# Output projection of a hybrid encoder layer on one Trainium2 core: where two weight blocks, two scale rows and the last two kept units are loaded, and in which order they are split

## The chip, the cores and the metric

The kernel runs on one core of one Trainium2 chip, in one launch. Times are device microseconds. A core has five engines with a queue each: TensorE (PE in the profile, its weight loads PEld), VectorE (DVE), ScalarE (ACT), GpSimd (POOL) and SyncE (SP). Loads and stores are issued here by SP and by POOL; 16 DMA engines carry them out. An instruction starts when its turn in its engine's queue has come and the semaphores that it waits for are reached.

## The reference

One layer of a streaming encoder for 384 tokens (256 of a new stream, 8 x 16 of running streams), in three token blocks of 128. All numbers are float32. The part around the change:

```python
merged = (gates[:, :, 0] * br_pool + gates[:, :, 1] * br_ssd).astype(u.dtype)
out = merged @ p['w_out']                      # (384 x 2048) @ (2048 x 2048)
...
x = x + rmsnorm(m, p['g_mix_post'])            # m is out
hdn = jnp.square(jax.nn.relu(rmsnorm(x, p['g_mlp_pre']) @ p['w_up'])) @ p['w_down']
x = x + rmsnorm(hdn, p['g_mlp_post'])
```

`merged` comes out of a pooling branch and a state-space branch; the change touches neither. It lies between the last product of those branches (`w_ssd`) and the first of the MLP (`w_up`).

## The kernel before

**Precision.** Every float32 product is done as three products of rounded parts: a weight tile `w` is split into a high part `wh` (ScalarE, a copy) and a low part `wl` (VectorE, the difference), and so are the tokens' tiles. `mm` issues high by high, high by low, low by high (L151 to L153; L1208 to L1210 in the blocks). A split of a 128 x 1024 weight tile is one instruction of ACT and one of DVE behind it.

**The output projection** has four blocks of 512 columns.

- Block 2 is computed plainly by `moving` (L142): eight units `wo2_0` to `wo2_7` of 1024 columns, each loaded by SP into a `w` buffer, split, and multiplied with all three token blocks, 18 matmuls a unit.
- Blocks 0 and 1 are computed together by `seven` (L1177), in two calls, one for each half of the inner dimension. It replaces eight block products by seven on sums of blocks. Four weight blocks of 1 MB (W11, W12, W21, W22, called `W[0]`, `W[3]`, `W[2]`, `W[4]` in the code, loads `o_w` from `w_os`) and two sums of them (`wsum`, DVE) are split in halves named a to g; the sums of the token tiles (`S0` to `S7`, loads `w_S` from `s_scr`, by `ssplit`) go in on the other side. `evict` brings results to `hm`, and in the second call `settle` squares them (ACT) and scales them with the gain row (DVE).
- Block 3 is again plain: units `wo3_0` to `wo3_2` ahead of the second `seven`, and `wo3_3` to `wo3_7` kept: split by `keep` into tiles `eh`, `el` of pool `phk` at the end of the second `seven`, and multiplied after it for one token block after the other, 6 matmuls a unit and block. `finish3` then squares, norms (`postnorm`) and adds the residual `x1`; ahead of the last two units of the third token block eight transposes of the new `x1` stand in TensorE's queue (`first_turns`).

**Buffers.** Pool `wpool` has three buffers for each of `w`, `wh` and `wl`. A load into `w` waits until the split of the tile three loads earlier is done; a split into `wh` and `wl` waits until TensorE has left the tile three splits earlier. Units, `S` tiles and the MLP's weights take turns in `w`. `phs` (`px`) holds the six blocks, two split tiles and the splits of S; it is closed in the second `seven`, and `pg0` and `phk` take its memory, tile by tile as the last readers leave.

**What sets the order.** The engines' queues hold the instructions in an order that a scheduler finds from the program; `behind(x)` (`issue_after`) puts what follows behind instruction `x` in that order, `later()` behind the last split. TensorE's order is chained by `last[0]`. `fetch[0]` is the last unit load of `wfetch` (L64).

**Lines that the change touches.** `gains` (L1122) loads a gain row of 512 to all partitions through POOL and scales it by -0.5 on ACT; for blocks 0 and 1 it puts the row into unused parts of `hm` (L1330), for 2 and 3 into the tile `gpo`. `prep` (L1148) loads a block through POOL, `prep_late` (L1151) through SP: W21 behind unit 3 of block 2 and W22 behind unit 4 (hooks, L1326 and L1327). `seven` from L1273 opens `phk`, splits the first three kept units, settles, evicts (L1285), then loads and splits the last two (L1289), and settles again. `second` (L1341) runs the second `seven`.

Of the kernel before, what the change touches and what calls it, by code (L numbers as in the profile page):

```python
# [6 lines left out]
F32 = mybir.dt.float32  # L7
# [7 lines left out]
P = 128  # L15
# [18 lines left out]
def build(ctx, tc, io):  # L34
# [23 lines left out]
    def behind(ins):  # L58
        return nullcontext() if ins is None else tc.issue_after(ins.ins)
# [4 lines left out]
    def wfetch(src, name):  # L64
        w = wpool.tile([P, 1024], F32, tag="w", name=f"w_{name}")
        fetch[0] = sy.dma_start(w, src)
        return w, name
# [69 lines left out]
    def keep(tile, f):  # L137
        w, name = f
        h, l = tile
        return s.activation(h, w, AF.Copy), v.tensor_tensor(l, w, h.bitcast(F32), ALU.subtract)  # L140
# [901 lines left out]
    with tc.tile_pool(name="phf", bufs=1, side="right", reuse_waits="tile") as pf, tc.tile_pool(  # L1042
# [77 lines left out]
            lo(range(4), False)  # L1120

        def gains(nb, gpo=None):  # L1122
            if gpo is None:
                gpo = pf2.tile([P, 512], F32, tag="gpo", name=f"gpo{nb}", bufs=1)
            gp.dma_start(gpo, io["g_mix_post"][blk(nb)].partition_broadcast(P))
            s.activation(gpo, gpo, AF.Copy, scale=-0.5)
            return gpo

# [21 lines left out]

        def prep_late(i):  # L1151
            with behind(fetch[0]):
                sy.dma_start(W[(0, 3, 2, 4)[i]], io["w_os"][0, i])

        def wsum(out, a, b):
            for q in both:
# [20 lines left out]
        def seven(c):  # L1177
# [34 lines left out]
            def settle():  # L1212
                with behind(low[0]), behind(high[0]):
                    while due:
                        b, j, src = due.pop(0)
                        squared(b, j, src)
                        scaled(b, j, src, gains01[j])
# [55 lines left out]
            if c:  # L1273
                phs.close()
                pg0 = xin.enter_context(tc.tile_pool(name="pg0", bufs=1, reuse_waits="tile"))
                xtiles(pg0, NE)
                pk = phk.enter_context(tc.tile_pool(name="phk", bufs=1, reuse_waits="tile"))
                for i in reversed(range(5)):
                    kept[i] = [pk.tile([P, 1024], F32R, name=f"e{n}_wo3_{3 + i}") for n in "hl"]
                with behind(low[0]):  # L1280
                    for i in range(3):
                        high[0], low[0] = keep(kept[i], kf[i])
            run(g1, (2, 3), (X, 2, False))
            settle()
            evict(0, 0, X, first=True, done=True)  # L1285
            if c:
                with behind(low[0]):
                    for i in (3, 4):
                        _, low[0] = keep(kept[i], wfetch(*tail3[i]))  # L1289
            settle()  # L1290

        def finish3(b):
# [25 lines left out]
        def added(*w):  # L1318
            def go():
                with later():  # L1320
                    wsum(*w)

            return go

        hooks = {k: (lambda k=k: ssplit(k)) for k in range(4)}
        hooks[3] = lambda: (ssplit(3), prep_late(2))  # L1326
        hooks[4] = lambda: prep_late(3)  # L1327
        hooks[5] = added(1, 0, 3)
        moving(o, [(io["w_out"][0, kp], f"wo2_{kp}") for kp in range(8)], ms_, 0, done2, hook=hooks)
        gains01 = [gains(0, hm[:, 2, blk(3)]), gains(1, hm[:, 1, blk(3)])]  # L1330
        seven(0)
        blocks(1)
        for i in range(4):
# [7 lines left out]
        def second():  # L1341
            with later():
                wsum(5, 1, 4)
            kf.extend(wfetch(*u) for u in tail3[:3])
            with behind(fetch[0]):
                for b in range(3):
                    sy.dma_start(x1[:, b, :], io["x_tok"][b])
            seven(1)
            gpo3.append(gains(3))
# [563 lines left out]
```

## Time and profile before

| | |
|---|---|
| time, median of 3 runs | 2614.03 us (2613.3 to 2614.59) |
| the profiled execution: its own time | 2614.43 us |
| the profiled execution: span, first to last instruction | 2612.7 us |
| granted TensorE clock, mean | 0.999 |
| DMA, mean | 177 GB/s |
| plain units of block 2 | 1514.3 to 1547.1 us |
| first and second `seven` with units 0 to 2 of block 3 between | 1547.1 to 1615.8 us |
| kept units of block 3, for three token blocks | 1615.8 to 1639.4 us |

A line of the profile names the engine, the line of the kernel, the operation and output<-input, with buffer numbers left out: `wl_wo` is the low part of any plain unit of blocks 2 and 3, `el_wo` that of a kept unit, `o_w` any of the weight blocks, `w_S` a token sum, `trm` a transpose. SPq marks an issue of a load by SP; how long the load took is told apart from it, as us from issue to landing. In a timeline each line has start, duration, and in brackets how long the engine was idle ahead of it and who released it.

### The profile page before, as it was taken

What the parts mean: (1) busy time and instruction counts of PE and PEld (TensorE: products, weight loads), DVE (VectorE), ACT (ScalarE), POOL (GpSimd) and SP (SyncE); (2) the same over time, 40 slices, a digit from 0 to 9 for tenths busy, and PEclk for the clock granted to TensorE, in tenths of its full rate; (3) what the DMA queues carried; (4) which work ended last, traced back from release to release, by engine and by line L of the source; (5) the groups of instructions that cost most, each with busy time, mean ns of one, the idle gap of its engine ahead of it and who ended that gap; (6) DMA issues with size and microseconds to landing.
All of it is one profiled execution on the core that took longest, in us unless ns stands there. A gap on an engine that the chain in (4) does not pass through costs nothing.

```text
span 2612.7 us, 40398 instructions
## 1 busy us (share of the span) xinstructions
PE 2598.7 (99%) x15977; PEld 2500.8 (96%) x15977; DVE 1827.1 (70%) x2468; ACT 1323.4 (51%) x2008; POOL 196.7 (8%) x284
## 2 busy tenths in 40 slices
PE   9999999999999999999999999999999999999998
PEld 9999999999999999999999988999999999999997
DVE  6685334788888888876544468766676868677677
ACT  6443324666566565744333345645454545454454
POOL 0000000001111111120100000000000000000000
PEclk9999999999999999999999999999999999999999
DMA  7444445566766576666655565543433444444444
GB/s 284 143 136 155 149 146 203 183 205 208 232 210 223 198 240 201 218 215 233 215 172 167 165 213 186 217 138 129 142 132 129 157 158 142 141 146 137 137 143 144
DMA packets 139886, 463.28 MB, mean 177 GB/s; under 512 B 17712, under 2 KB 44912, under 8 KB 125232
## 3 DMA queue, kind: packets, MB, share of 16 engines
q1 hardware_dynamic: 115536, 321.99, 38.3%
q0 software_dynamic: 24160, 138.70, 14.6%
q8 instruction: 126, 2.06, 0.3%
q14 instruction: 64, 0.52, 0.1%
HBM read 412.88 MB, written 47.75 MB: 176 GB/s over the span
## 4 chain that ended last, share of the span: by engine, by line
PE 95%; DVE 1%; DMA 1%; ACT 1%; issue 1%; SPq 0%; DVEq 0%; POOL 0%; ACTq 0%; POOLq 0%
PE pj_up L101 6%; PE pj_up L102 6%; PE pj_up L103 6%; PE pj_x L101 5%; PE pj_x L103 4%; PE pj_x L102 4%; PE pj_sp L103 3%; PE pj_sp L102 3%; PE pj_sp L101 3%; PE pj_z L103 3%; PE pj_z L102 3%; PE pj_z L101 3%; PE X L1619 2%; PE c L1619 2%; PE c L1618 2%; PE c L1617 2%
## 5 line engine op out<-in xcount | busy, mean ns | idle before, releaser
L101 PE MATMUL pj_up<-x1h,wh_up 128*128 128x384 f32 (+1 forms) x1024 | 333.9, 326 | 0.0
L103 PE MATMUL pj_up<-x1h,wl_up 128*128 128x384 f32 (+1 forms) x1024 | 333.7, 326 | 0.0
L102 PE MATMUL pj_up<-x1l,wh_up 128*128 128x384 f32 (+1 forms) x1024 | 333.7, 326 | 0.0
L101 PE MATMUL pj_x<-xgh,wh_x 128*128 128x384 f32 x768 | 251.9, 328 | 0.0
L103 PE MATMUL pj_x<-xgh,wl_x 128*128 128x384 f32 x768 | 250.5, 326 | 0.3 <-DVE wl_x L74 0.3
L102 PE MATMUL pj_x<-xgl,wh_x 128*128 128x384 f32 x768 | 250.4, 326 | 0.0
L73 ACT ACTIVATE wh_up<-w_up 128x1024 fp32r<-128x1024 f32 x126 | 133.1, 1056 | 186.7 <-PE pj_up L102 110.7
L74 DVE TENSOR_TENSOR wl_up<-w_up,wh_up 128x1024 fp32r<-128x1024 f32 x126 | 154.0, 1223 | 57.7 <-ACT wh_up L73 56.9
L102 PEld LDWEIGHTS pj_up<-x1l,wh_up 128*128 128x128 f32 x1024 | 193.5, 189 | 0.4
L101 PEld LDWEIGHTS pj_up<-x1h,wh_up 128*128 128x128 f32 x1024 | 193.5, 189 | 0.4
L103 PEld LDWEIGHTS pj_up<-x1h,wl_up 128*128 128x128 f32 x1024 | 193.5, 189 | 0.0
L103 PE MATMUL pj_z<-xgh,wl_z 128*128 128x384 f32 x512 | 167.0, 326 | 0.2 <-DVE wl_z L74 0.2
L101 PE MATMUL pj_sp<-abh,wh_sp 128*128 128x384 f32 x512 | 166.9, 326 | 0.0
L102 PE MATMUL pj_sp<-abl,wh_sp 128*128 128x384 f32 x512 | 166.9, 326 | 0.0
L103 PE MATMUL pj_sp<-abh,wl_sp 128*128 128x384 f32 x512 | 166.9, 326 | 0.0
L102 PE MATMUL pj_z<-xgl,wh_z 128*128 128x384 f32 x512 | 166.9, 326 | 0.0
L101 PE MATMUL pj_z<-xgh,wh_z 128*128 128x384 f32 x512 | 166.9, 326 | 0.0
L73 ACT ACTIVATE wh_x<-w_x 128x1024 fp32r<-128x1024 f32 x96 | 100.9, 1052 | 107.0 <-PE pj_z L102 53.0
L74 DVE TENSOR_TENSOR wl_x<-w_x,wh_x 128x1024 fp32r<-128x1024 f32 x96 | 117.4, 1223 | 52.7 <-ACT wh_x L73 52.7
L74 DVE TENSOR_TENSOR wl_sp<-w_sp,wh_sp 128x1024 fp32r<-128x1024 f32 x64 | 78.3, 1223 | 108.4 <-ACT wh_sp L73 108.4
L73 ACT ACTIVATE wh_sp<-w_sp 128x1024 fp32r<-128x1024 f32 x64 | 67.8, 1059 | 166.3 <-PE pj_sp L102 158.2
L101 PEld LDWEIGHTS pj_x<-xgh,wh_x 128*128 128x128 f32 x768 | 145.1, 189 | 2.3 <-issue 0.4
(583 smaller groups left out, 7190.4 us busy)
## 6 DMA issues: line engine op xcount, KB each, us to landing
w_up<-w_up SPq DMA_DIRECT2D x128, 512.0 KB, 3.4
w<-w_dn POOLq DMA_DIRECT2D x60, 1024.0 KB, 5.2
w_x<-w_in SPq DMA_DIRECT2D x96, 512.0 KB, 4.0
w_z<-w_in SPq DMA_DIRECT2D x64, 512.0 KB, 3.5
w_sp<-w_ssd SPq DMA_DIRECT2D x64, 512.0 KB, 3.5
w_ga<-w_ga SPq DMA_DIRECT2D x32, 512.0 KB, 3.5
w_pp<-w_pp SPq DMA_DIRECT2D x32, 512.0 KB, 3.4
hs<-ssm POOLq DMA_DIRECT2D x16, 1024.0 KB, 7.2
```

The lines of the kernel that those rows point to most:

```text
L73: cut[0] = s.activation(h, w, AF.Copy)
L74: cut[1] = v.tensor_tensor(l, w, h.bitcast(F32), ALU.subtract)
L101: te.matmul(out, wh, xh, start=first, stop=False, **how)
L102: te.matmul(out, wh, xl, start=False, stop=False, **how)
L103: return te.matmul(out, wl, xh, start=False, stop=last, **how)
L1617: te.matmul(o, h[:, t], vh, start=go, stop=False, skip_group_check=True)
L1618: te.matmul(o, h[:, t], vl, start=False, stop=False, skip_group_check=True)
L1619: last[0] = te.matmul(o, l[:, t], vh, start=False, stop=False, skip_group_check=True)
```

## The change

1. W21 and W22 of the first `seven` are no longer loaded behind units 3 and 4 of block 2, but both behind unit 5's hook, and `prep_late` now moves `fetch[0]`, so that each load stands behind the one before.
2. The gain rows of blocks 0 and 1 are loaded in `second`, ahead of the loads of kept units 3 to 5, through SP and behind `fetch[0]`, no longer through POOL during the plain units.
3. The last two kept units, `wo3_6` and `wo3_7`, get `w` tiles of their own in `phk`, loaded when `phk` is opened, where they took `w` buffers of `wpool` before.
4. In the second `seven` the `settle` between the last products and the last eviction is left out, so the two last splits stand directly behind that eviction, and the rest is settled after them.

```diff
         def gains(nb, gpo=None):
+            src = io["g_mix_post"][blk(nb)].partition_broadcast(P)
             if gpo is None:
                 gpo = pf2.tile([P, 512], F32, tag="gpo", name=f"gpo{nb}", bufs=1)
-            gp.dma_start(gpo, io["g_mix_post"][blk(nb)].partition_broadcast(P))
+                gp.dma_start(gpo, src)
+            else:
+                with behind(fetch[0]):
+                    sy.dma_start(gpo, src)
             s.activation(gpo, gpo, AF.Copy, scale=-0.5)
             return gpo
...
         def prep_late(i):
             with behind(fetch[0]):
-                sy.dma_start(W[(0, 3, 2, 4)[i]], io["w_os"][0, i])
+                fetch[0] = sy.dma_start(W[(0, 3, 2, 4)[i]], io["w_os"][0, i])
...
                     kept[i] = [pk.tile([P, 1024], F32R, name=f"e{n}_wo3_{3 + i}") for n in "hl"]
+                for i in (3, 4):
+                    w = pk.tile([P, 1024], F32, name=f"w_wo3_{3 + i}")
+                    sy.dma_start(w, tail3[i][0])
+                    kf.append((w, tail3[i][1]))
                 with behind(low[0]):
                     for i in range(3):
                         high[0], low[0] = keep(kept[i], kf[i])
             run(g1, (2, 3), (X, 2, False))
-            settle()
+            if not c:
+                settle()
             evict(0, 0, X, first=True, done=True)
             if c:
                 with behind(low[0]):
                     for i in (3, 4):
-                        _, low[0] = keep(kept[i], wfetch(*tail3[i]))
+                        _, low[0] = keep(kept[i], kf[i])
             settle()
...
-        hooks[3] = lambda: (ssplit(3), prep_late(2))
-        hooks[4] = lambda: prep_late(3)
-        hooks[5] = added(1, 0, 3)
+        sum0 = added(1, 0, 3)
+        hooks[5] = lambda: (sum0(), prep_late(2), prep_late(3))
...
-        gains01 = [gains(0, hm[:, 2, blk(3)]), gains(1, hm[:, 1, blk(3)])]
+        gains01 = []
...
             with later():
                 wsum(5, 1, 4)
+            gains01[:] = [gains(0, hm[:, 2, blk(3)]), gains(1, hm[:, 1, blk(3)])]
             kf.extend(wfetch(*u) for u in tail3[:3])
```

TensorE's queue holds the same instructions in the same order. The other engines' queues move at three places.

SP during the plain units of block 2 (`wo2`), up to the first units of block 3 (`wo3`). Before:

```order
L1161 DMA w_S2_15768<-s_scr2_165 128x640
L66 DMA w_wo2_5_15774<-w_out 128x1024
L1153 DMA o_w21_0_15672<-w_os 128x2048
L1161 DMA w_S3_15798<-s_scr3_166 128x640
L66 DMA w_wo2_6_15805<-w_out 128x1024
L1153 DMA o_w22_0_15671<-w_os 128x2048
L66 DMA w_wo2_7_15830<-w_out 128x1024
L66 DMA w_wo3_0_16119<-w_out 128x1024
L66 DMA w_wo3_1_16125<-w_out 128x1024
L66 DMA w_wo3_2_16131<-w_out 128x1024
```

With the change:

```order
L1165 DMA w_S2_15768<-s_scr2_165 128x640
L66 DMA w_wo2_5_15774<-w_out 128x1024
L1165 DMA w_S3_15798<-s_scr3_166 128x640
L66 DMA w_wo2_6_15804<-w_out 128x1024
L66 DMA w_wo2_7_15828<-w_out 128x1024
L1157 DMA o_w21_0_15672<-w_os 128x2048
L1157 DMA o_w22_0_15671<-w_os 128x2048
L66 DMA w_wo3_0_16115<-w_out 128x1024
L66 DMA w_wo3_1_16121<-w_out 128x1024
L66 DMA w_wo3_2_16127<-w_out 128x1024
L1129 DMA hm_15661<-g_mix_post 128x512 x2
```

W21 (`o_w21`) and W22 (`o_w22`) have moved from behind units 5 and 6 of block 2 to behind its last unit, and the two gain rows (`hm<-g_mix_post`), on POOL before, stand behind unit 2 of block 3.

ACT at the same place; `oc`, `ob` and `oa` are the first splits of the first `seven`, `st1` takes the sums of squares. Before:

```order
L1164 ACTIVATE Sh2_15770<-w_S2_15768 128x640
L1126 ACTIVATE gpo2_15678<-gpo2_15678 128x512
L1126 ACTIVATE hm_15661<-hm_15661 128x512
L73 ACTIVATE wh_wo2_5_15776<-w_wo2_5_15774 128x1024
L1126 ACTIVATE hm_15661<-hm_15661 128x512
L1164 ACTIVATE Sh3_15800<-w_S3_15798 128x640
L73 ACTIVATE wh_wo2_6_15807<-w_wo2_6_15805 128x1024
L73 ACTIVATE wh_wo2_7_15832<-w_wo2_7_15830 128x1024
L1195 ACTIVATE wh_oc0_0_15909<-o_w1_0_15674 128x1024
L1195 ACTIVATE wh_ob0_0_15931<-o_w21_0_15672 128x1024
L1134 ACTIVATE hm_15661,st1_15662<-wo2_0_15681 128x512
```

With the change:

```order
L1168 ACTIVATE Sh2_15770<-w_S2_15768 128x640
L1130 ACTIVATE gpo2_15678<-gpo2_15678 128x512
L73 ACTIVATE wh_wo2_5_15776<-w_wo2_5_15774 128x1024
L1168 ACTIVATE Sh3_15800<-w_S3_15798 128x640
L73 ACTIVATE wh_wo2_6_15806<-w_wo2_6_15804 128x1024
L73 ACTIVATE wh_wo2_7_15830<-w_wo2_7_15828 128x1024
L1199 ACTIVATE wh_oc0_0_15905<-o_w1_0_15674 128x1024
L1199 ACTIVATE wh_ob0_0_15927<-o_w21_0_15672 128x1024
L1130 ACTIVATE hm_15661<-hm_15661 128x512 x2
L1138 ACTIVATE hm_15661,st1_15662<-wo2_0_15681 128x512
L1138 ACTIVATE hm_15661,st1_15662<-wo2_1_15682 128x512
L1138 ACTIVATE hm_15661,st1_15662<-wo2_2_15683 128x512
```

The two scalings of the gain rows (`hm<-hm`) have moved from around unit 5 to ahead of the evictions of block 2.

DVE at the end of the second `seven`, from the third kept split on; `n0` to `n3` are the small tiles of the first token block's norm, `up` the MLP's first weights. Before:

```order
L140 TENSOR_TENSOR el_wo3_5_16449<-w_wo3_5_16225,eh_wo3_5_16448 128x1024
L1130 TENSOR_TENSOR hm_15661<-oB_15905,hm_15661 128x512
L1130 TENSOR_TENSOR hm_15661<-hm_15661 128x512
L1224 TENSOR_TENSOR hm_15661<-hm_15661,oX1_16230 128x512
L140 TENSOR_TENSOR el_wo3_6_16447<-w_wo3_6_16471,eh_wo3_6_16446 128x1024
L1018 TENSOR_TENSOR n0_n10_16515<-st1_15662 128x1
L1019 TENSOR_TENSOR n0_n10_16515<-n0_n10_16515,st1_15662 128x1
L1020 TENSOR_SCALAR n0_n10_16515<-n0_n10_16515 128x1
L140 TENSOR_TENSOR el_wo3_7_16445<-w_wo3_7_16475,eh_wo3_7_16444 128x1024
L1130 TENSOR_TENSOR hm_15661<-hm_15661 128x512
L74 TENSOR_TENSOR wl_up0_0_16676<-w_up0_0_16673,wh_up0_0_16675 128x1024
L1022 TENSOR_SCALAR n1_n10_16516<-st1_15662,n0_n10_16515 128x1
```

With the change:

```order
L140 TENSOR_TENSOR el_wo3_5_16449<-w_wo3_5_16225,eh_wo3_5_16448 128x1024
L1228 TENSOR_TENSOR hm_15661<-hm_15661,oX1_16230 128x512
L140 TENSOR_TENSOR el_wo3_6_16447<-w_wo3_6_16454,eh_wo3_6_16446 128x1024
L140 TENSOR_TENSOR el_wo3_7_16445<-w_wo3_7_16456,eh_wo3_7_16444 128x1024
L1134 TENSOR_TENSOR hm_15661<-oB_15901,hm_15661 128x512
L1134 TENSOR_TENSOR hm_15661<-hm_15661 128x512 x2
L1018 TENSOR_TENSOR n0_n10_16515<-st1_15662 128x1
L74 TENSOR_TENSOR wl_up0_0_16676<-w_up0_0_16673,wh_up0_0_16675 128x1024
L1019 TENSOR_TENSOR n0_n10_16515<-n0_n10_16515,st1_15662 128x1
L74 TENSOR_TENSOR wl_up1_0_16682<-w_up1_0_16679,wh_up1_0_16681 128x1024
L1020 TENSOR_SCALAR n0_n10_16515<-n0_n10_16515 128x1
L74 TENSOR_TENSOR wl_up0_1_16688<-w_up0_1_16685,wh_up0_1_16687 128x1024
```

The eviction of the last products and the splits of units 6 and 7 have moved ahead of the settling of the rest; all three splits of the MLP's first weights stand ahead of the norm's next step, `n1`, where before one stood ahead of it, one ahead of the reciprocal, and one behind the residuals. On ACT the splits and settlings stand in the matching order, and on SP the loads of units 6 and 7 keep their place, behind the `x1` rows and ahead of the `w_up` loads.

## The prediction

> **What bounds the kernel now.** First the page, busy time by engine, beside the span in the table above.
>
> ```profile
> PE 2598.7 (99%) x15977; PEld 2500.8 (96%) x15977; DVE 1827.1 (70%) x2468; ACT 1323.4 (51%) x2008; POOL 196.7 (8%) x284
> ```
>
> TensorE is busy for all but 14 us of the span, and the change leaves its instructions and their order as they are. Time can only come from places where TensorE stands still. The second view is the list of its waits, cut to the output projection and what follows it, 1505 to 1660 us (releaser, us in total, times, longest).
>
> ```profile
> PE wo L152 <- DVE el_wo L140: 1.5, 2, 0.8
> PE wo L152 <- DVE wl_wo L74: 0.8, 1, 0.8
> PE trm L1080 <- DVE x L1065: 0.5, 1, 0.5
> ```
>
> Three places: a weight split in the plain units (wl_wo), two in the kept units (el_wo), and one transpose. From 1652 us to the end the same view is empty. The third view, busy time by stretch, gives the size. I cut it at the first matmul of block 2's plain units (1514.30), of the seven products (1547.10), of the kept units (1615.80), and behind the last kept unit.
>
> ```profile
> 1514.30:1547.10 32.80, 31.61 (x146) 27.15 (x145) 17.91 (x22) 14.93 (x20) 2.15 (x4) 1.00 0.80 279
> 1547.10:1615.80 68.70, 68.70 (x319) 60.01 (x318) 63.04 (x64) 41.21 (x54) 2.66 (x5) 1.00 0.42 154
> 1615.80:1639.40 23.60, 21.32 (x99) 17.59 (x99) 20.14 (x38) 11.72 (x22) 0.96 (x2) 1.00 0.65 222
> ```
>
> The columns are length, busy PE, PEld, DVE, ACT, POOL, granted clock, DMA share, GB/s. Plain units: 1.19 us idle, at a DMA share of 0.80. The seven products: none. Kept units: 2.28 us idle. The clock is 1.00 throughout, so a gap costs its own length. The real loss is larger than the idle time, since a matmul's modelled 0.38 us hides part of a gap; I measure from start to start, against the undisturbed 0.216 us (68.70 us for 319 recorded matmuls). A plain unit is 18 matmuls, 3.89 us; a kept unit is 6 for each token block, 1.30 us.
>
> **The first stall, unit 6 of block 2.** TensorE's timeline, then SP's issues, ACT's split of that unit, and the DMA view of 1519 to 1537 us (KB each, median us from issue to landing).
>
> ```profile
> 1537.41 0.38 PE L153 MATMUL wo<-wh_wo,ml 128*128 128x512 f32 x1
> 1538.19 0.48 PE L151 MATMUL wo<-wh_wo,mh 128*128 128x512 f32 x1 [0.41 <-ACT wh_wo L73]
> 1539.45 0.48 PE L152 MATMUL wo<-wl_wo,mh 128*128 128x512 f32 x1 [0.78 <-DVE wl_wo L74]
> 1539.77 0.38 PE L153 MATMUL wo<-wh_wo,ml 128*128 128x512 f32 x1
> ```
>
> ```profile
> 1520.79 0.33 SPq L1161 DMA_DIRECT2D w_S<-s_scr  x1
> 1521.53 0.33 SPq L66 DMA_DIRECT2D w_wo<-w_out  x1
> 1521.90 0.51 SPq L1153 DMA_DIRECT2D o_w<-w_os  x1
> 1525.48 0.33 SPq L1161 DMA_DIRECT2D w_S<-s_scr  x1
> 1530.50 0.33 SPq L66 DMA_DIRECT2D w_wo<-w_out  x1
> ```
>
> ```profile
> 1537.08 1.06 ACT L73 ACTIVATE wh_wo<-w_wo 128x1024 fp32r<-128x1024 f32 x1 [2.31 <-DMA w_wo<-w_out]
> ```
>
> ```profile
> o_w<-w_os SPq DMA_DIRECT2D x2, 1024.0 KB, 10.0
> w_S<-s_scr SPq DMA_DIRECT2D x2, 320.0 KB, 8.3
> hm<-g_mix_post POOLq DMA_DIRECT2D x2, 256.0 KB, 8.5
> ```
>
> Three steps take 2.36 us instead of 0.65: **1.71 us lost**. Followed back: ACT split unit 6 at 1537.08, when it landed, 6.6 us after its issue at 1530.50. It was issued that late because it takes the buffer of S2, and S2, issued at 1520.79, needed some 8 us, with two scale rows (256 KB each, POOL, 8.5 us) and a weight block (1 MB, SP, 1521.90, 10 us) in flight beside it.
>
> The change takes just these loads out. From S2's issue to its landing there remain the scale row of block 2, unit 5 and S2 itself, 1.1 MB instead of 2.6; at this stretch's 279 GB/s that is 4 us instead of 9. I take S2 landed at 1525, its split done by 1526.6, unit 6 issued there and landed at 1533.2 at the latest (its 6.6 us again). Its two splits (1.06 and about 1.2 us) end by 1535.6. TensorE wants unit 6 at 1514.30 + 6 x 3.89 = 1537.6, 2 us later, so the whole 1.71 us go. Bounds: 0 (S2 stays late) and 1.71.
>
> What is late next: the two weight blocks, W21 and W22, now go out behind unit 7, whose buffer is free when unit 5 is split, about 1528.5. The split wh_ob needs W21, but also a buffer that TensorE leaves with unit 6, at 1541.5; at 10 us W21 is there by 1539. W22 is used only after the first nine splits of the seven products, some 8 us on. I take 0; the cover is 2.5 us for W21. If it were late, TensorE would wait from 1549.3 on (18 matmuls into the seven products), so another 5 us are in hand.
>
> The scale rows now go through SP behind unit 2 of block 3, which takes the buffer of unit 7. The split of unit 7 waits until TensorE leaves unit 4 (1514.30 + 5 x 3.89 = 1533.8) and ends at 1536.2, so the rows are issued at about 1536.7. Of the 4.7 MB issued from 1528.5 on (W21, W22, four units, two rows), at 279 GB/s the last lands at 1545.4; by the 8.5 us for such a row, at 1545.2. Their two scalings on ACT now stand ahead of block 2's evictions, which wait for TensorE until 1545.4 in any case. I take 0; its price if it fails is the third rival. Nearer rows for such a row on SP there are none, and below 0 it cannot go, since nothing waited for the rows before.
>
> [...] No row of before shows a scale row on SP.
>
> **The second stall, units 6 and 7 of block 3 (kept).** TensorE's timeline, SP's issue of both loads, and ACT's split of unit 6; then the first use of S4's split by wh_of.
>
> ```profile
> 1619.51 0.38 PE L153 MATMUL wo<-eh_wo,ml 128*128 128x512 f32 x1
> 1620.17 0.48 PE L151 MATMUL wo<-eh_wo,mh 128*128 128x512 f32 x1 [0.29 <-ACT eh_wo L140]
> 1621.43 0.48 PE L152 MATMUL wo<-el_wo,mh 128*128 128x512 f32 x1 [0.78 <-DVE el_wo L140]
> 1621.76 0.38 PE L153 MATMUL wo<-eh_wo,ml 128*128 128x512 f32 x1
> ...
> 1622.62 0.38 PE L151 MATMUL wo<-eh_wo,mh 128*128 128x512 f32 x1
> 1623.74 0.48 PE L152 MATMUL wo<-el_wo,mh 128*128 128x512 f32 x1 [0.74 <-DVE el_wo L140]
> 1624.06 0.38 PE L153 MATMUL wo<-eh_wo,ml 128*128 128x512 f32 x1
> ```
>
> ```profile
> 1615.47 1.46 SPq L66 DMA_DIRECT2D w_wo<-w_out  x2
> ```
>
> ```profile
> 1619.06 1.06 ACT L140 ACTIVATE eh_wo<-w_wo 128x1024 fp32r<-128x1024 f32 x1 [3.94 <-DMA w_wo<-w_out]
> ```
>
> ```profile
> L1208 PE MATMUL oY<-wh_of,Sh x4: 379/379/379, 1609.4 to 1612.6; 128*128 128x512 f32 x4
> ```
>
> Unit 6: 2.25 us for three steps, 1.60 lost. Unit 7: 1.44 for two, 1.01 lost. **Together 2.61 us.** The loads went out at 1615.47, when the split of unit 3 freed a buffer, and ACT stood 3.94 us for the first. In tiles of their own they wait for the readers of the memory that phs leaves. By the pools' order of allocation unit 6's tile lies over the second half of W11, split early, and unit 7's over S4's split, which the first oY products with wh_of read last, from 1609.4. So unit 7, the later one, goes out near 1610.2 in the clock of before; with the 3.6 us of the first load (1615.47 to 1619.06) it is there at 1614.
>
> Then the new order of ACT and DVE decides. DVE's rows of before, and the transposes that end the stretch:
>
> ```profile
> 1614.21 3.50 DVE L140 TENSOR_TENSOR el_wo<-w_wo,eh_wo 128x1024 fp32r<-128x1024 f32 x3
> 1617.61 0.70 DVE L1130 TENSOR_TENSOR hm<-oB,hm 128x512 f32<-128x512 f32 x1
> 1618.21 0.69 DVE L1130 TENSOR_TENSOR hm<-hm 128x512 f32<-128x512 f32 x1
> ```
>
> ```profile
> 1628.46 0.16 DVE L1023 RECIPROCAL n_n<-n_n 128x1 f32<-128x1 f32 x1 [0.38 <-ACT n_n L1021]
> ```
>
> ```profile
> 1635.28 0.27 PE L1080 MATMUL trm<-cst,x 128*128 128x128 f32 x1
> 1636.02 0.98 PE L1080 MATMUL trm<-cst,x 128*128 128x128 f32 x7 [0.47 <-DVE x L1065]
> ```
>
> A 1024-wide split advances DVE by 1.13 us (3.40 from 1614.21 to 1617.61 for three), a 512-wide step by 0.60. The new order: three el to 1617.6, one eviction to 1618.2, el of unit 6 to 1619.4, el of unit 7 to 1620.5. TensorE wants them at 1615.80 + 3 x 1.30 + 0.22 = 1619.9 and 1.3 later, 1621.2: 0.5 and 0.7 us in hand, both waits go. Then three 512-wide steps to 1622.3, three wl_up, 1024 wide as well (the first MLP weights), with four small sums between them (3.4 + 0.8), and the reciprocal of the first norm at 1626.5, 2.0 us earlier than 1628.46. (ACT's root comes with TensorE, 2.61 earlier, and is not last.) One of the three wl_up stood behind the reciprocal and ahead of the transposes, so the transposes can go 2.0 + 1.1 = 3.1 us earlier, at 1632.9. TensorE gets to them 13 kept pieces x 1.296 after 1615.80, at 1632.65, to the second of them 0.1 later, and waits 0.2 where it lost 0.64 (0.74 less one step of 0.1). **0.43 us more.** Bounds 0 and 0.64.
>
> From there the rest hangs on TensorE as before, and no wait follows to the end that could give the gain back.
>
> **Sum.** 1.71 + 2.61 + 0.43 = 4.75 us; 4.3 to 5.0 if both stalls go. The profiled execution took 2614.43 us (1.7 around its span), less 4.75 is 2609.7; the median shown is 0.4 below that execution, so **2609.3 us**. About 0.2% (5.2 us) is what a measurement of this kernel can tell from no change; the sum stays just under it.
>
> **Rivals.** *DVE becomes the bound of the kept units.* For it: DVE is busy 20.14 of 23.60 us there. If the evictions and wl_up that now stand ahead of the norm take all that the early splits give, TensorE waits at the transposes for what it gained, and only the first 1.71 us remain: **2612.3 us**. Against it: 3.5 us of idle DVE in that stretch. Chance 0.11.
>
> *The change does not free S2.* Unit 4, unit 5 and the scale row of block 2 still share the queues; unit 6 stays late and only the kept units gain, 3.04 us: **2611.0 us**. Against it: 2 us in hand. Chance 0.08.
>
> *The other side: the scale rows hold ACT.* Their scalings stand ahead of the three evictions and wh_oa, and TensorE needs wl_oa. Before:
>
> ```profile
> 1546.32 0.58 ACT L1134 ACTIVATE hm<-wo 128x512 f32<-128x512 f32 x1
> ```
>
> ```profile
> 1549.57 1.22 DVE L1196 TENSOR_TENSOR wl_oa<-o_w,wh_oa 128x1024 fp32r<-128x1024 f32 x1
> ```
>
> ```profile
> L1208 PE MATMUL oX<-wh_oa,mh x6: 379/379/379, 1553.6 to 1597.1; 128*128 128x512 f32 x6
> ```
>
> First eviction to the end of wl_oa is 4.5 us, two scalings ahead about 1.1. TensorE needs wl_oa at 1553.6 + 0.2 - 1.7 = 1552.1, so a landing later than 1546.5, 9.8 us after issue, delays it one for one. At 14.6 us the gain is gone, and from 19.8 us the kernel is over 0.2% slower: **2619.3 us** and up. The 1 MB blocks took 10 us in that traffic, so the loss of a microsecond can be, of ten hardly. [...] Chance 0.05.
>
> **How the numbers follow.** Forecast 0.76, rivals 0.11, 0.08 and 0.05. Of the forecast's 0.76 I put 0.17 beyond 5.2 us, since the three runs of before spread over 1.3 us and 4.75 is 0.5 from that bound. So faster 0.17, same 0.79, slower 0.04 (the last rival less its mildest end). The range 2608.3 to 2612.4 takes in the sum's bounds, with most of that spread below them, and the two rivals that gain less.
>
> **What would show it.** Right: no wait for wl_wo, wh_wo, el_wo or eh_wo in TensorE's list; S2 lands in 4 to 5 us; the loads of units 6 and 7 are issued before 1610; the wait at the transposes is under 0.3 us. Wrong: ACT's scalings of hm standing for their DMA so long that wl_oa or wl_ob reaches TensorE, or a new wait of TensorE for DVE between 1610 and 1640.

## The result and the profile after

| | before | changed |
|---|---|---|
| time, median of 22 runs each | 2613.82 us (2612.25 to 2614.85) | 2609.95 us (2609.38 to 2610.57) |
| the profiled execution: its own time | 2614.43 us | 2610.17 us |
| its span | 2612.7 us | 2608.4 us |

The ratio is 0.9985, with an interval of 0.9979 to 0.9992: 3.87 us less, and between 2.1 and 5.5 us by the interval. Forecast were 4.75 us less and 2609.3 us; the time lies in the stated range, and the change stays below the 0.2% (5.2 us) that the prediction named as its bound.

First the same views as before the change: TensorE's busy time on the page, and the list of all waits of TensorE, now over the whole span (releaser, us in total, times, longest).

```profile
PE 2597.8 (100%) x15977; PEld 2501.3 (96%) x15977; DVE 1826.3 (70%) x2468; ACT 1323.3 (51%) x2008; POOL 195.7 (8%) x282
```

```profile
PE warm_o L234 <- DVE warm L230: 1.2, 1, 1.2
PE pj_p L101 <- ACT wh_e L295: 0.4, 1, 0.4
PE pj_z L103 <- DVE wl_z L74: 0.2, 1, 0.2
```

These three lie at the start of the program. Nothing of wl_wo, el_wo or the transposes is left. Then busy time by stretch, cut at the same four matmuls (length, busy PE, PEld, DVE, ACT, POOL, granted clock, DMA share, GB/s).

```profile
1514.90:1546.00 31.10, 31.10 (x146) 27.24 (x145) 18.90 (x22) 14.23 (x17) 1.08 (x2) 1.00 0.82 295
1546.00:1614.60 68.60, 68.60 (x319) 60.09 (x318) 62.18 (x63) 43.19 (x59) 2.66 (x5) 1.00 0.48 169
1614.60:1635.20 20.60, 20.45 (x99) 17.72 (x99) 19.60 (x37) 10.31 (x21) 0.89 (x2) 1.00 0.56 204
```

The plain units take 31.10 us where they took 32.80, with no idle PE, and the kept units 20.60 where they took 23.60 for the same 99 recorded matmuls. In the plain units the DMA engines are as busy as before (a share of 0.82 against 0.80): what changed is the order of the loads. Around unit 6 of block 2, SP's issues and ACT's splits of S2 and of unit 6:

```profile
1521.40 0.33 SPq L1165 DMA_DIRECT2D w_S<-s_scr  x1
1522.23 0.33 SPq L66 DMA_DIRECT2D w_wo<-w_out  x1
1526.05 0.33 SPq L1165 DMA_DIRECT2D w_S<-s_scr  x1
1529.32 2.42 SPq L66 DMA_DIRECT2D w_wo<-w_out  x2
1531.79 0.90 SPq L1157 DMA_DIRECT2D o_w<-w_os  x2
```

```profile
1527.69 0.74 ACT L1168 ACTIVATE Sh<-w_S 128x640 fp32r<-128x640 f32 x1 [2.93 <-DMA w_S<-s_scr]
...
1532.91 1.07 ACT L73 ACTIVATE wh_wo<-w_wo 128x1024 fp32r<-128x1024 f32 x1 [1.46 <-DMA w_wo<-w_out]
```

S2 still takes 6.3 us from issue to split (1521.40 to 1527.69), not 4. Unit 6 goes out at 1529.32, which is 14.4 us after the first plain matmul where it was 16.2, and its load takes 3.6 us, not 6.6. The scale rows and what they hold, SP's issue and then ACT:

```profile
1538.20 0.83 SPq L1129 DMA_DIRECT2D hm<-g_mix_post  x2
```

```profile
1545.07 1.21 ACT L1130 ACTIVATE hm<-hm 128x512 f32<-128x512 f32 x2 [1.64 <-DMA hm<-g_mix_post]
1546.19 0.58 ACT L1138 ACTIVATE hm<-wo 128x512 f32<-128x512 f32 x1
```

ACT stands 1.64 us for the rows and evicts block 2 at 1546.19, when TensorE has just left it (1546.00). The end of the output projection, the issue of the two kept loads (SP), their splits (ACT), DVE from the first el_wo on, and TensorE at the transposes:

```profile
1590.68 18.65 SPq L1286 DMA_DIRECT2D w_wo<-w_out  x2
```

```profile
1612.57 1.06 ACT L140 ACTIVATE eh_wo<-w_wo 128x1024 fp32r<-128x1024 f32 x1
...
1614.13 1.06 ACT L140 ACTIVATE eh_wo<-w_wo 128x1024 fp32r<-128x1024 f32 x1
```

```profile
1613.02 3.49 DVE L140 TENSOR_TENSOR el_wo<-w_wo,eh_wo 128x1024 fp32r<-128x1024 f32 x3
1616.43 0.68 DVE L1228 TENSOR_TENSOR hm<-hm,oX 128x512 f32<-128x512 f32 x1
1617.03 2.35 DVE L140 TENSOR_TENSOR el_wo<-w_wo,eh_wo 128x1024 fp32r<-128x1024 f32 x2
...
1625.35 0.16 DVE L1023 RECIPROCAL n_n<-n_n 128x1 f32<-128x1 f32 x1 [0.44 <-ACT n_n L1021]
```

```profile
1631.47 1.40 PE L1080 MATMUL trm<-cst,x 128*128 128x128 f32 x8
1632.63 0.46 PE L151 MATMUL wo<-eh_wo,mh 128*128 128x512 f32 x1
```

The two loads go out at 1590.68 and near 1609.0 (the row's end less its last issue), long before 1615.47. Neither eh_wo waits for a DMA, el of unit 6 and 7 follow the last eviction in one row, and the eight transposes run without a break.

### The profile page after: what moved, and what is told of

It is laid out like the page before. It is cut to its first block, busy times and chain, and to the rows that moved or that the text cites. A ratio compares the mean times of both kernels' runs of the same rounds, so it can differ in the third digit from the quotient of the medians.

```text
span 2608.4 us, 40397 instructions
## 1 busy us (share of the span) xinstructions
PE 2597.8 (100%) x15977; PEld 2501.3 (96%) x15977; DVE 1826.3 (70%) x2468; ACT 1323.3 (51%) x2008; POOL 195.7 (8%) x282
## 4 chain that ended last, share of the span: by engine, by line
PE 97%; DVE 1%; ACT 1%; DMA 0%; issue 0%; SPq 0%; DVEq 0%; ACTq 0%
PE pj_up L102 6%; PE pj_up L101 6%; PE pj_up L103 6%; PE pj_x L101 5%; PE pj_x L102 5%; PE pj_x L103 5%; PE pj_sp L103 3%; PE pj_sp L101 3%; PE pj_sp L102 3%; PE pj_z L103 3%; PE pj_z L101 3%; PE pj_z L102 3%; PE c L1628 2%; PE X L1628 2%; PE c L1627 2%; PE X L1627 2%
```

## The experiments

All kernels are compared with the kernel before on the same chip. The profiled executions are compared by four stretches, each from one first matmul to the next: the plain units; the seven products with units 0 to 2 of block 3; the kept units up to the first matmul behind the transposes; and from there to the last matmul, 966.94 to 966.98 us in every one. So whatever differs behind the first plain matmul differs in the three columns here. That matmul itself starts between 1513.55 and 1515.54 us in the fourteen profiles. The last column is the median time less that of before in the same comparison, good to some 2.4 us either way. By the times alone only the changed kernel, e4, e6 and e7 differ from before; for the others the stretches have to say it, and each of them is from one profile.

| kernel | plain units | seven products | kept units | time less before's |
|---|---|---|---|---|
| before, the three profiles | 32.80, 31.53, 32.91 | 68.73, 68.66, 68.71 | 20.92, 20.89, 21.23 | |
| changed, the two profiles (e5 the second) | 31.08, 31.08 | 68.64, 68.94 | 17.99, 18.00 | -3.87, -3.66 |
| e1_only_w | 31.08 | 68.63 | 20.85 | -0.97 |
| e2_only_gain | 31.08 | 70.66 | 21.01 | +0.89 |
| e3_first_half | 31.08 | 69.81 | 20.75 | -0.92 |
| e4_second_half | 32.57 | 68.63 | 18.01 | -3.05 |
| e6_w_and_kept | 31.21 | 68.63 | 18.00 | -3.65 |
| e7_scale_later | 31.08 | 68.64 | 18.00 | -3.83 |
| e8_rows_three_times | 31.08 | 74.69 | 18.01 | +0.80 |
| e9_only_tiles | 32.63 | 68.64 | 18.49 | -2.10 |
| e10_only_order | 33.07 | 68.64 | 21.12 | +0.30 |

### The two blocks alone: e1_only_w

```diff
         def prep_late(i):
             with behind(fetch[0]):
-                sy.dma_start(W[(0, 3, 2, 4)[i]], io["w_os"][0, i])
+                fetch[0] = sy.dma_start(W[(0, 3, 2, 4)[i]], io["w_os"][0, i])
...
-        hooks[3] = lambda: (ssplit(3), prep_late(2))
-        hooks[4] = lambda: prep_late(3)
-        hooks[5] = added(1, 0, 3)
+        sum0 = added(1, 0, 3)
+        hooks[5] = lambda: (sum0(), prep_late(2), prep_late(3))
```

> W21 and W22 behind unit 7, the scale rows still on POOL during the plain units, kept units as before. Theory A (the prediction's: the traffic around S2 makes unit 6 late, because S2's split frees its buffer): S2 still shares the DMA engines with the scale rows and stays near 8 us, unit 6 is still issued near 1530, and at most half of the 1.7 us goes; 0 to 0.9 us less than before. Theory B (the 1 MB block that stands ahead of unit 6 on SP makes unit 6's own load slow, 6.6 us instead of the 3.6 us that the changed kernel shows): unit 6 is issued as late as before, lands in about 3.6 us, and the stall at unit 6 is gone; 1.7 us less than before.

2613.29 us against 2614.26, ratio 0.9995 (0.9986 to 1.0004): by the time alone not to be told from no change, so the trace has to say it. SP's issue of unit 6, then ACT's splits of S2 and of unit 6:

```profile
1530.92 2.73 SPq L66 DMA_DIRECT2D w_wo<-w_out  x2
```

```profile
1529.30 0.74 ACT L1164 ACTIVATE Sh<-w_S 128x640 fp32r<-128x640 f32 x1 [4.78 <-DMA w_S<-s_scr]
...
1534.60 1.06 ACT L73 ACTIVATE wh_wo<-w_wo 128x1024 fp32r<-128x1024 f32 x1 [1.42 <-DMA w_wo<-w_out]
```

The first stall is gone in full (31.08), and yet S2 is as late as before (issued at 1521.00, split at 1529.30: 8.3 us), so unit 6 goes out as late as before. What changed is its own load: 3.7 us instead of 6.6. In the kernel before, two blocks lie beside it, and e1 takes both away. W22 is issued on SP 0.38 us behind unit 6 (1530.88 behind 1530.50). W21 is issued ahead of it, and takes 11.4 us to land, as the DMA view of before for 1521.80 to 1522.00 us shows (KB, us from issue to landing):

```profile
o_w<-w_os SPq DMA_DIRECT2D x1, 1024.0 KB, 11.4
```

So W21 is under way until 1533.3, 2.8 us after unit 6 goes out. The prediction had the right place and the wrong load; which of the two blocks it is, a load in e6 tells further down.

### The scale rows alone: e2_only_gain

```diff
         def gains(nb, gpo=None):
...
+            else:
+                with behind(fetch[0]):
+                    sy.dma_start(gpo, src)
...
-        gains01 = [gains(0, hm[:, 2, blk(3)]), gains(1, hm[:, 1, blk(3)])]
+        gains01 = []
...
+            gains01[:] = [gains(0, hm[:, 2, blk(3)]), gains(1, hm[:, 1, blk(3)])]
             kf.extend(wfetch(*u) for u in tail3[:3])
```

> Only the scale rows move to SP behind unit 2 of block 3; W21 and W22 stay behind units 3 and 4. Theory A: S2 comes 2 to 4 us earlier, unit 6 is issued near 1527, lands by 1534 even at 6.6 us, and the stall at unit 6 is gone; 1.7 us less than before. Theory B: unit 6's load still stands behind W21 and takes over 6 us; some of the stall stays, 0.5 to 1.5 us less than before.

2615.15 us, 1.0002 (0.9993 to 1.0011). Without the rows unit 6 lands in time too, with W21 still ahead of it and W22 still behind: its load takes 4.3 us, so the plain units lose nothing. S2 has little to do with it (7.6 us from issue to split instead of 8.1). But the seven products lose 2.0 us, which neither theory foresaw. Their waits, TensorE's list from 1505 to 1660 us:

```profile
PE oX L1212 <- ACT hm L1226: 0.5, 1, 0.5
PE oX L1213 <- DVE wl_od L1200: 0.3, 1, 0.3
...
PE oB L1213 <- DVE wl_oe L1200: 0.2, 1, 0.2
```

The rows are issued only at 1541.15 here, ACT scales them at 1545.34, and wh_ob, the evictions and wh_oa all stand behind them in ACT's queue; the delay comes out 13 to 18 us on, at wl_od, wl_oe and a result that ACT evicts. This is the prediction's third rival at work in one part of the change, giving back what another part had won.

### Parts 1 and 2 together: e3_first_half

The edits of the two runs above in one kernel.

> Both loads moved, kept units as before. Both theories: no wait of TensorE in the plain units, the kept units' waits as before (2.6 us lost, and about 0.6 at the transposes): 1.7 to 1.8 us less than before, from the first plain unit to the first kept unit 99.7 us instead of 101.5.

2613.34 us, 0.9997 (0.9988 to 1.0006). The plain units are undisturbed, the seven products lose 1.17 us: the rows are issued at 1539.41, scaled at 1546.23, 0.35 us after TensorE has begun the seven products (1545.88). So it is 100.89 us up to the first kept unit and not the 99.7 that were expected. In the time that loss isn't seen (e1, without it, took 2613.29). TensorE's list has the last two of the three waits again:

```profile
PE oX L1213 <- DVE wl_od L1200: 0.3, 1, 0.3
PE oB L1213 <- DVE wl_oe L1200: 0.2, 1, 0.2
```

### Parts 3 and 4 together: e4_second_half

```diff
+                for i in (3, 4):
+                    w = pk.tile([P, 1024], F32, name=f"w_wo3_{3 + i}")
+                    sy.dma_start(w, tail3[i][0])
+                    kf.append((w, tail3[i][1]))
...
-            settle()
+            if not c:
+                settle()
             evict(0, 0, X, first=True, done=True)
...
-                        _, low[0] = keep(kept[i], wfetch(*tail3[i]))
+                        _, low[0] = keep(kept[i], kf[i])
```

> Kept units with tiles of their own and the settling behind their splits; the plain units as before. Prediction: the stall at unit 6 of block 2 stays (1.7 us), no wait for eh_wo or el_wo, 2.9 to 3.0 us less than before, from the first kept unit to the end of the transposes 18.0 us instead of 20.9. Rival (DVE is the bound of the kept units): under 1 us less than before, with a longer wait at the transposes.

2611.21 us, 0.9988 (0.9979 to 0.9997). The kept units take 18.01 us, all that the whole change has there, and the first stall stays (32.57). So the two halves are separate: -0.92 and -3.05 sum to -3.97, the whole change measured -3.87, with intervals of 1.7 to 2.4 us either way.

### The changed kernel again, and without the rows ahead of the evictions: e5, e6, e7

The profile of the changed kernel had 4.74 us less in the three stretches, its time 3.87. These three ask whether the scalings on ACT cost the rest. e5 is the changed kernel without an edit. e6 has the rows on POOL during the plain units again, as before; against the changed kernel:

```diff
-            else:
-                with behind(fetch[0]):
-                    sy.dma_start(gpo, src)
+            gp.dma_start(gpo, io["g_mix_post"][blk(nb)].partition_broadcast(P))
...
-        gains01 = []
+        gains01 = [gains(0, hm[:, 2, blk(3)]), gains(1, hm[:, 1, blk(3)])]
```

e7 leaves the rows on SP and puts the scalings behind the last split; against the changed kernel:

```diff
-            s.activation(gpo, gpo, AF.Copy, scale=-0.5)
+            with later() if nb < 2 else nullcontext():
+                s.activation(gpo, gpo, AF.Copy, scale=-0.5)
```

> The changed kernel itself, beside the next three on one chip. Theory C (new: the two scalings hold ACT, and with it the evictions of block 2 and the DVE work up to the split of block sum d; TensorE waits there once the scale rows land later than about 1545.5): the profile of the changed kernel was just inside the edge, other executions are outside; 3.5 to 4.5 us less than before, and where its profile has the rows landed after 1545.6, a wait of TensorE for wh_od or wl_od. Theory D (the 0.9 us between the trace's 4.75 and the timed 3.87 lie in how executions begin, ahead of the projection): no such wait whatever the landing, and the first plain unit starts up to 1 us later in slower executions.

> The changed kernel with the scale rows back on POOL during the plain units. Theory C: no scaling ahead of the evictions, no wait in the seven products; unit 6 has 0.5 to 1 us in hand as in the run with only the weight blocks moved; 4.5 to 4.8 us less than before, and 0.5 to 1 us less than the changed kernel beside it. Theory D: as the changed kernel, within 0.3 us.

> The changed kernel, only the two scalings of the scale rows stand on ACT behind the split of S4, ahead of the second seven products, where ACT waits for loads anyway. Theory C: no wait of TensorE from the first plain unit to the end; 4.7 us less than before and 0.5 to 1 us less than the changed kernel. Theory D: as the changed kernel, within 0.3 us.

2610.06 us (ratio 0.9987, 0.9978 to 0.9996), 2610.07 (0.9987, 0.9978 to 0.9995) and 2609.89 (0.9986, 0.9977 to 0.9995). The three agree within 0.2 us: taking the scalings from ahead of the evictions brings no 0.9 us. So the scalings do not account for the 0.9 us; in the profiles they cost 0.30 us in e5 and nothing in the first one. e6 shows besides that part 2 isn't needed: with the rows on POOL as before, S2 needs 7.9 us, unit 6 still 3.6, and the time is that of the whole change.

e6 also tells the two blocks apart. Unit 7 of block 2 goes out there at 1534.22 (the first row's end less its last issue), with W21 0.38 us and W22 0.85 us behind it. SP, then ACT's split of unit 7 when it lands:

```profile
1530.86 3.69 SPq L66 DMA_DIRECT2D w_wo<-w_out  x2
1534.60 0.90 SPq L1153 DMA_DIRECT2D o_w<-w_os  x2
```

```profile
1537.83 1.06 ACT L73 ACTIVATE wh_wo<-w_wo 128x1024 fp32r<-128x1024 f32 x1 [2.32 <-DMA w_wo<-w_out]
```

The load takes 3.6 us (1534.22 to 1537.83), no more than unit 6 ahead of it. In the seven profiles with the blocks moved, unit 7 takes 3.5 to 4.5 us with both blocks behind it. So blocks issued behind a load delay it by 1 us at most here, and what is left for unit 6 of before is W21, issued ahead of it and still under way. (S3 and the second row are under way at that moment in e6 as well, and unit 6 takes 3.6 us there.) In the seven profiles with the blocks in their old places W21 lands 2.1 to 3.0 us after unit 6 goes out, and unit 6 takes 4.3 to 6.6 us; in the seven with the blocks moved it takes 3.5 to 3.7. No run moves W21 alone, so this is argued from the traces and not tested by a change.

### The rows loaded three times: e8_rows_three_times

```diff
             else:
                 with behind(fetch[0]):
-                    sy.dma_start(gpo, src)
+                    for _ in range(3):
+                        sy.dma_start(gpo, src)
```

Each of the two rows is loaded three times into the same place, one load behind the other.

> The changed kernel with each scale row loaded three times one after the other into its place, so that it lands later, about 1550 to 1554, with everything else as it was. Theory C: TensorE waits in the first seven products one for one, landing less 1545.5, some 5 to 8 us, and the kernel is 1 to 4 us slower than before. Theory D: nothing but the loads' own 1 MB of traffic, within 0.5 us of the changed kernel. The prediction's third rival had the edge at 1546.5 and the same slope.

2614.52 us, 1.0006 (0.9996 to 1.0015): the whole gain is lost. ACT, TensorE's list, and busy time of two stretches, cut where the granted clock changes (columns as above):

```profile
1551.82 0.63 ACT L1131 ACTIVATE hm<-hm 128x512 f32<-128x512 f32 x1 [5.35 <-DMA hm<-g_mix_post]
1552.36 1.04 ACT L1200 ACTIVATE wh_oc<-o_w 128x1024 fp32r<-128x1024 f32 x1
1553.30 0.63 ACT L1131 ACTIVATE hm<-hm 128x512 f32<-128x512 f32 x1
```

```profile
PE oY L1213 <- ACT wh_oc L1200: 0.9, 1, 0.9
PE oY L1214 <- DVE wl_oc L1201: 0.8, 1, 0.8
PE oM L1214 <- DVE wl_ob L1201: 0.6, 1, 0.6
```

```profile
1552.19:1555.52 3.33, 1.67 (x6) 0.67 (x4) 1.83 (x2) 3.22 (x5) 0.00 (x0) 1.00 0.62 257
1555.52:1562.35 6.83, 6.26 (x16) 4.89 (x16) 6.38 (x6) 2.56 (x3) 0.00 (x0) 0.50 0.01 2
```

ACT stands 5.35 us for the first row with wh_oc and wh_ob behind it, and the seven products take 6.05 us more than 68.64. Only about half of that is waiting: the three waits cost 2.8 us from start to start. The other half is the clock. From 1555.52 to 1562.35 the granted clock is 0.50, and the 15 matmul steps from 1556.19 to 1562.32 take 6.13 us instead of 3.24. The fall comes behind the first two waits, when TensorE had been busy for 1.67 of 3.33 us; in none of the other thirteen profiles does the granted clock fall before 2600 us (its mean over the span is 0.999 in each of them and 0.997 here). So theory C's 5 to 8 us came out, but its "one for one" did not: a part of the number is luck. (Here the order that the scheduler found has the evictions ahead of the scalings; the weight splits are what is held.) No later split passed the scaling that waited: wh_oc starts 8.8 us after the first eviction (1543.54 to 1552.36), where e7, with the scalings behind the last split, has it 3.9 us after (1545.53 to 1549.41).

### The kernel before, profiled twice more

No edit. Two theories were left for the 0.9 us: that the first stall of before is not the same in every execution, or that only the start of the program differs.

> The kernel before, unchanged, profiled once more. Theory E (the loss at plain unit 6 of block 2 differs from one execution to the next, with the landing of that unit's load): the stretch from the first matmul of that group's plain units to its first kept unit is not 101.53 us again but anywhere from 99.7 to 103 us, and the stretch from there to the first matmul after the transposes stays at 20.9. Theory F (the loss is the same in every execution, and only the start of the program differs): 101.5 +- 0.2 us and 20.9, with the group's start anywhere from 1513.5 to 1515.5.

> The kernel before, unchanged, a third profile, with the same two theories as for the second: E, a stretch between 99.7 and 103 us that differs from that of the other two profiles by over 0.3 us in at least one of them; F, 101.5 +- 0.2 us in all three.

SP's issue of unit 6, ACT's split of it, and TensorE's wait in the second profile:

```profile
1530.91 0.33 SPq L66 DMA_DIRECT2D w_wo<-w_out  x1
```

```profile
1536.33 1.06 ACT L73 ACTIVATE wh_wo<-w_wo 128x1024 fp32r<-128x1024 f32 x1 [1.24 <-DMA w_wo<-w_out]
```

```profile
1538.70 0.48 PE L152 MATMUL wo<-wl_wo,mh 128*128 128x512 f32 x1 [0.19 <-DVE wl_wo L74]
```

The load takes 5.4 us here (1530.91 to 1536.33) against 6.6 and 6.1 in the other two, and the stall is 0.45 us against 1.72 and 1.83. In six profiles with the blocks and rows in their old places (before three times, e4, e9, e10) the plain units take 31.53 to 33.07 us, the loss following the split of unit 6 one for one: it begins when that split starts later than 21.0 us after the first plain matmul (1536.33 - 1514.83 = 21.50 gives 0.45; 1537.08 - 1514.31 = 22.77 gives 1.72). So the first theory holds, and the start differs besides (1514.06 to 1514.83). The profile shown before the prediction had a stall (1.72 us) above the mean of these six, 1.5 us.

### Parts 3 and 4 apart: e9_only_tiles and e10_only_order

e9 has the tiles and early loads of part 3 and keeps the `settle` ahead of the eviction:

```diff
+                for i in (3, 4):
+                    w = pk.tile([P, 1024], F32, name=f"w_wo3_{3 + i}")
+                    sy.dma_start(w, tail3[i][0])
+                    kf.append((w, tail3[i][1]))
...
-                        _, low[0] = keep(kept[i], wfetch(*tail3[i]))
+                        _, low[0] = keep(kept[i], kf[i])
```

e10 leaves that `settle` out and keeps the loads as they were:

```diff
-            settle()
+            if not c:
+                settle()
             evict(0, 0, X, first=True, done=True)
```

> The two kept units' tiles and early loads alone, with all three roundings ahead of them kept on VectorE. If the loads are what held TensorE: both waits at the kept units go, the stretch from the first kept unit to the matmul after the transposes is 18.0 to 18.4 us, and the time is that of the second half, 2611.2. If the place of the three roundings matters as well: el6 and el7 stand behind three roundings of some 0.6 us on VectorE, so a part of the wait stays, the stretch is 19 to 20 us, and the time some 2612.3.

> The rounding left out ahead of the kept units alone, with their loads where they were before. If the loads are what held TensorE: both waits stay, the stretch from the first kept unit to the matmul after the transposes is 20.5 to 20.9 us, and the time is 2613.4 to 2613.9. If VectorE's order matters as much as the loads: a stretch of 19 to 20 us and some 2612.3.

2611.61 us (0.9992, 0.9983 to 1.0001) and 2614.01 us (0.9999, 0.9990 to 1.0009). DVE and TensorE in e9:

```profile
1618.11 0.68 DVE L1130 TENSOR_TENSOR hm<-oB,hm 128x512 f32<-128x512 f32 x1
1618.71 0.68 DVE L1130 TENSOR_TENSOR hm<-hm 128x512 f32<-128x512 f32 x1
1619.31 0.68 DVE L1224 TENSOR_TENSOR hm<-hm,oX 128x512 f32<-128x512 f32 x1
1619.90 2.35 DVE L140 TENSOR_TENSOR el_wo<-w_wo,eh_wo 128x1024 fp32r<-128x1024 f32 x2
```

```profile
1621.17 0.48 PE L152 MATMUL wo<-el_wo,mh 128*128 128x512 f32 x1 [0.59 <-DVE el_wo L140]
```

The tiles alone bring the kept units from 20.92 to 18.49 us. Two settling steps (L1130; the first takes oB), 0.60 us each, stand ahead of oX's eviction and so of el of unit 6, and TensorE waits 0.59 for it; with the order changed as well the last 0.49 us go. The order alone brings nothing (21.12 us): with the loads issued at 1615.48 as before, ACT and DVE have nothing to split earlier. So it was mainly the loads that held TensorE: 18.49 is just above the 18.0 to 18.4 expected for that, and well below the 19 to 20 expected if the order weighed as much.

## Why the prediction was right, and where it was wrong

**The three places and their sizes: right.** In the profile that the prediction was made from, the stretches lose 1.72 (plain units) and 2.93 us (kept units) by the change, 4.65 together, and 0.09 in the seven products. Predicted were 1.71 and 2.61 + 0.43 = 3.04. No named wait came in their place. That the trace's 4.74 us meet the predicted 4.75 so closely is in part luck: the kept units gave 0.11 less, the seven products 0.09 that the sum did not have, and the first stall is of a size that changes from execution to execution. The wait of 0.2 us that the prediction left at the transposes is named in e4, e6, e7 and e8 and in neither profile of the changed kernel; the stretch is 17.99 to 18.01 us in all six.

**"I take S2 landed at 1525": wrong step, right outcome.** S2 was split at 1527.69, 6.3 us after its issue, where the division of 1.1 MB by 279 GB/s gave 4. The rate held (292 GB/s from 1521.40 to 1527.67), but that is 1.8 MB: the step counted three loads and left out what else was under way, as unit 4, a store of a token sum and S3. So the sign "S2 lands in 4 to 5 us" did not come. Unit 6 did go out 1.8 us earlier. The step that did more was taken as unchanged: "landed at 1533.2 at the latest (its 6.6 us again)". That load took 3.5 to 3.7 us in every kernel with W21 and W22 moved away. e1 and e6 show that this was enough of a cause, with S2 as late as ever; the rival "the change does not free S2" was right about S2 in those two kernels and wrong that unit 6 would then stay late.

Had the load taken its 6.6 us again, the split of unit 6 would have begun 21.0 us after the first plain matmul in the changed kernel, right at the edge found above, and 21.5 us after it in e5, past the edge. By this estimate the mechanism as predicted had nothing in hand where 2 us were stated, and that the whole 1.71 us went is luck as far as the reasoning goes.

The block that made the load slow is W21, ahead of it, as far as the traces tell (e6). e2 shows a second way: without the rows on POOL W21 landed after 10.1 us instead of 11.4, unit 6 took 4.3 us and was in time. So a load of 512 KB took 4.3 to 6.6 us (unit 6) with the block ahead of it and 3.5 to 4.5 (unit 7) with the two behind it; how the block ahead holds it is not shown, as no run here looks inside the queue.

**The kept units' loads and DVE's order: right.** "Near 1610.2 in the clock of before" was 1609.0 for the second load, on a clock on which the kept units begin 1.2 us earlier: the same place. Predicted on before's clock, where the kept units begin at 1615.80, and measured on that of after, where they begin at 1614.64, the pair of el began at 1618.2 and 1617.03, the reciprocal came at 1626.5 and 1625.35: 2.4 and 10.7 us after the first kept unit in both.

**The scale rows at 0: nearly right, with less in hand than stated.** The rows were issued at 1538.20 against a predicted 1536.7 (the plain units began 0.6 us later here), and ACT went on 6.9 us after that, not 8.5, so the landing came out close to the predicted one. The prediction put the edge at a landing of 1546.5, 1.1 us after TensorE leaves block 2. By the scalings' start against that moment, the changed kernel has 0.93 us before it (loss 0), e5 0.51 before it (loss 0.30 in the seven products), e3 0.35 after it (1.17). By these three the edge is some 0.8 us before that moment, two microseconds earlier than predicted. The step took wl_oa as what would come out late; what came late in e2 and e3 was wl_od and wl_oe, further down the same queue. Between the three the loss grows one for one with the lateness, as the rival said. e2 and e8, where other splits stood behind the scalings, are not on that line, and in e8 the halved clock (0.50 for 6.83 us) adds to the loss: "The clock is 1.00 throughout, so a gap costs its own length" held for the waits of before and not for those of e8.

**The time: 0.65 us off.** The sum was set against one profiled execution, whose first stall was 1.72 us. Over the three profiles of before the three stretches are 122.45, 121.08 and 122.85 us, 122.13 in the mean; over the two of the changed kernel 117.71 and 118.02, 117.87 in the mean. That is 4.26 us, of which 3.87 were measured, with an interval of 2.1 to 5.5. A varying stall accounts for half of the difference in these numbers. Another 0.3 us may lie ahead of the projection, which began at 1514.40 in the mean of the three and at 1514.72 in that of the two; five profiles are too few to say. The rest is far inside the interval and stays open.

## What to carry to other kernels

A load that is late may be late by its neighbours in the queue and not by its issue (unit 6: 6.6 us in before and 3.7 in e1, issued as late in both): before moving what delays the issue, compare the load's own duration with that of the same load in quiet, and look for a large transfer issued ahead of it that has not landed yet. Loads that wait only for a shared buffer should get memory that is free early, and then the order on the engine that splits them decides the rest; either alone was worth less (2.43 and 0 of 2.9 us here). A stall that ends with a DMA is a sample of one in one profile (1.72, 0.45 and 1.83 us here in three): take a second profile before it goes into a sum. Waits that follow each other closely may cost more than their length: in e8 three waits cost 2.8 us, and the granted clock of 0.50 that set in behind the first two, for 6.83 us, cost another 2.9; whether they caused it, one run does not show.

## What was not expected of the hardware

- A load of 512 KB took 3.5 to 3.7 us (unit 6) with no 1 MB load under way ahead of it, 3.5 to 4.5 us (unit 7) with two of 1 MB issued 0.38 and 0.85 us behind it, and 4.3 to 6.6 us (unit 6) with one of 1 MB that was issued earlier on SP and landed 2.1 to 3.0 us after its issue.
- The same load in the same kernel took 6.6, 5.4 and 6.1 us in three executions, though W21 landed 2.4 to 2.8 us after its issue in all three; what else differed stays open.
- Two waits of TensorE of 0.88 and 0.78 us, which end at 1553.45 and 1554.71, were followed by a granted clock of 0.50 from 1555.52 on for 6.83 us (e8), and that cost 2.9 us, as much as the waits themselves (2.8 us with the third). In the kernel before, waits of 0.29, 0.78 and 0.74 us, which end at 1620.17, 1621.43 and 1623.74, were not.
- A loss of 0.3 us can stand in no list of waits (e5: 68.94 us for the seven products, no wait named between 1505 and 1660 us) and show only in the distance from first matmul to first matmul.
